# Rows of 1/rms made elementwise from the sums on all partitions, in a hybrid encoder block on one core

## The chip, the core and the metric

The kernel runs on one core of one Trainium2 chip. The metric is the device time of one execution in microseconds (us); the kernel before takes 879.52 us, the median of three runs. The core has a matrix engine (TensorE, in the profile PE, its weight loads PEld), a vector engine (VectorE, DVE), an engine for functions by table (ScalarE, ACT), a general one (GpSimd, POOL) and one that issues DMAs (SyncE, SP). Each works through its own instructions in order and waits on semaphores for the others. On-chip data lie in SBUF; matmul results go to PSUM, which has banks of 128 partitions by 512 fp32 numbers.

## What is computed

One encoder block on x, 512 tokens by 1024 channels, in fp32. The normalisation is what the change touches:

```python
def rms_norm(x, g):
    xf = x.astype(F32)
    y = xf * lax.rsqrt(jnp.mean(xf * xf, axis=-1, keepdims=True) + EPS)   # EPS = 1e-6
    return (y * g.astype(F32)).astype(x.dtype)
```

The block is: h = rms_norm(x); one projection of h gives the inputs of three token mixers and of three merge gates. Mixer A is a bidirectional mLSTM (with a 3-tap convolution and silu on its q and k), B an attention within a neighbourhood, C a cross-attention into rms_norm(mem), with mem of 256 tokens. Each mixer is projected, multiplied by its sigmoid gate, summed, projected again and added to x. Then x plus a convolutional GLU network on rms_norm(x) (2816 hidden channels: a and u are two projections; gelu of the 3-tap convolution of a, times u, projected down), and a last rms_norm.

## The kernel before

**Layout.** Activations are kept with channels on partitions and tokens along the row, so 512 tokens are one row of 512 numbers, a full PSUM bank. The weights come in blocks of 128 by 1024, in the order in which they are used (`BLOCKS`), by DMAs from SP three blocks ahead (`RAW_AHEAD`, L147 and L159). One block ahead, each is split into a high and a low part: ScalarE writes the high part (L195), VectorE subtracts it and gives the low part (L196), each in two halves. A product of fp32 accuracy is then three matmuls, high by high, high by low, low by high (`mm3`, L213 to L215). `proj` (L395) does the 8 channel tiles of one output tile, 24 matmuls of 128x512; its argument `at` runs a function behind a given channel tile.

**The normalisations.** The gain g is multiplied into the activations when these are split. 1/rms depends on the token alone, so it is applied to the projections' results. For results with channels on partitions it has to be a row, the same on all 128 partitions (`rb`, 128x512); for those with tokens on partitions it is a column (`rc`, 128x4, one number for each token). It is made three times: for x, for mem (256 tokens) and for the second norm. The last norm has other code and is not touched.

1. The squares of the channel tiles are summed on 128 partitions: `acc` for x (L381 to L385), `macc` for mem (L485 to L492), `acc2` for the second norm (L1141 to L1145).
2. `two_parts` (L299) splits that sum, and `rstd_cols` (L305) multiplies both parts by a matrix of ones (L310). The result in PSUM holds each token's sum of squares on all 128 partitions.
3. `rstd_cols` then takes, 128 tokens at a time, the diagonal out of it: product with the identity, summed along the row, divided by 1024, epsilon added (L314). POOL raises that to the power -0.5 (L317), which is the column.
4. `row_parts` (L320) splits the column into a high part (ScalarE, L324) and a low part (VectorE, L325) and writes both back as diagonal matrices (L330, 128x128 each).
5. `rstd_row` (L334) multiplies the two by the matrix of ones (L339), which spreads each token's number over all partitions, and ScalarE copies the result out of PSUM (L341): the row.

For x the sums are issued inside the projection `mlk` 0 (L443), the row's matmuls inside `mlk` 1 (L444). The row is first read by `conv` (L456), which multiplies the four accumulated tiles `ps_q` of the mLSTM's q and the first two of its k by it, and goes on with L458 to L460 and the silu (L465, L466). The pool `mmp` has four PSUM banks, all held by `ps_q` up to there; `mlk` 2, the next projection, takes the first that comes free. The pool `atp` has four more (sums, rows, the first two k tiles, and the token tiles of the first `tm` block, L500 to L510). The column of x is multiplied by a constant (L448) and scales what is computed with tokens on partitions (L514 to L526).

For mem the sums are issued after the tile `("o", 1)` (L1035), the diagonals after `("o", 2)` (L1037), the row's matmuls within `("o", 3)` (L1021 to L1025). Row and column are read from the `memk` and `memv` tiles on (L1045, L1057). Around it the steps of the mLSTM run (`step`): decay factors by Exp (L710, L714), products with them (L715, L717), matmuls on these (L725, L727).

For the second norm the sums are issued behind the last channel tile of `ua` 0 (L1305), the row's matmuls within `uu` 1 (L1309). The row is read by `conv` (L456) and once more on POOL (L1319).

**The order.** A scheduler of the language lays out each engine's instructions; `tc.issue_after` holds an instruction behind a named one. The order of the lines is therefore not that of an engine, and a change in one helper can move others' instructions.

Of the kernel before, what the change touches and what calls it, by code (L numbers as in the profile page):

```python
# [11 lines left out]
F32 = mybir.dt.float32  # L12
# [5 lines left out]
P = 128  # L18
S = 512
# [91 lines left out]
def hybrid_block(ctx, tc, xg, xT, memT, wflat, vecs, gbias, nabias, outa, outb, outc):  # L111
# [14 lines left out]
    def nm(s):  # L126
        uid[0] += 1
        return f"{s}_{uid[0]}"
# [4 lines left out]
    def scr(n=512):  # L133
        return sp.tile([P, S], F32, tag="scr", name=nm("s"))[:, :n]

    def tiny(n):
        return tp.tile([P, 32], F32, tag="tiny", name=nm("y"), bufs=12)[:, :n]
# [4 lines left out]
    def atps():  # L142
        return atp.tile([P, 512], F32, tag="at", name=nm("at"))
# [158 lines left out]
        V.tensor_tensor(l, acc, h.bitcast(F32), op=ALU.subtract)  # L302
        return h, l

    def rstd_cols(parts, ntok, tag, n=D):  # L305

        nt = ntok // P
        ps = atps()
        for i in range(2):
            st["mm"] = PE.matmul(ps[:, :ntok], onesr, parts[i], start=i == 0, stop=i == 1).ins  # L310

        v, junk = tiny(nt), scr(P)
        for t in range(nt):
            V.tensor_tensor_reduce(junk, ps[:, t * P:(t + 1) * P], ident, 1.0 / n, EPS, ALU.mult, ALU.add,  # L314
                                   accum_out=v[:, t:t + 1])
        col = cp.tile([P, nt], F32, name=f"rc_{tag}")
        st["pool"] = G.tensor_tensor(col, v, nhalf[:, :nt], op=ALU.pow).ins  # L317
        return col

    def row_parts(col, ntok):  # L320

        nt = ntok // P
        ch, cl = tp.tile([P, 32], F32R, tag="tiny", name=nm("y"), bufs=12)[:, :nt], tiny(nt)
        A.activation(ch, col, AF.Copy)  # L324
        V.tensor_tensor(cl, col, ch.bitcast(F32), op=ALU.subtract)  # L325
        dgs = []
        for c in (ch.bitcast(F32), cl):
            dg = sp.tile([P, S], F32R, tag="scr", name=nm("s"))[:, :ntok]
            for t in range(nt):
                V.tensor_scalar(dg[:, t * P:(t + 1) * P], ident, c[:, t:t + 1], None, op0=ALU.mult)  # L330
            dgs.append(dg)
        return dgs

    def rstd_row(col, ntok, tag, parts=None):  # L334

        dgs = parts or row_parts(col, ntok)
        pb = atps()
        for n, dg in enumerate(dgs):
            PE.matmul(pb[:, :ntok], onesr, dg, start=n == 0, stop=n == 1)  # L339
        rb = cp.tile([P, ntok], F32, name=f"rb_{tag}", tag=f"rb{ntok}", bufs=1)  # L340
        A.activation(rb, pb[:, :ntok], AF.Copy)  # L341
        return rb


# [34 lines left out]
    def x_square(k):  # L379
        if k == 0:  # L380
            A.activation(acc, xk[k], AF.Square)  # L381
        else:
            sq = scr()
            A.activation(sq, xk[k], AF.Square)
            V.tensor_tensor(acc, acc, sq, op=ALU.add)  # L385

    norm = []
    late = []
# [6 lines left out]
    def proj(key, XHs, XLs, n=S, at={}, ps=None):  # L395

        ws = weights(key)
        k0 = 0 if ps is None else 1
        if ps is None:
            ps = mmps()  # L400
        for k in range(k0, KT):
            mm3(ps[:, :n], ws[k][0], ws[k][1], XHs[k], XLs[k], k == 0, k == KT - 1)
            if k == 1:
                flush()
            if k in at:
                at[k]()
        return ps
# [32 lines left out]
                mm3(ps_k[f], kh[:, fs], kl[:, fs], XH[0], XL[0], True, False)  # L440

    xsum = two_parts(acc, S)
    proj(("mlk", 0), XH, XL, ps=ps_k[0], at={1: lambda: norm.append(rstd_cols(xsum, S, "x"))})  # L443
    proj(("mlk", 1), XH, XL, ps=ps_k[1], at={4: lambda: norm.append(rstd_row(norm[0], S, "x"))})  # L444
    rc, rb = norm
    SY.dma_start(gbf, gbias.partition_broadcast(P))
    rcc = cp.tile([P, NT], F32, name="rcc")
    V.tensor_scalar(rcc, rc, C_ML, None, op0=ALU.mult)  # L448
# [31 lines left out]
    def mem_part(kp):  # L480

        t = scr()
        SY.dma_start(t.rearrange("p (k m) -> p k m", k=2), memT[:, 2 * kp:2 * kp + 2, :])
        sq = scr()
        A.activation(sq, t, AF.Square)  # L485
        for i in range(2):
            k = 2 * kp + i
            split_act(MH[k], ML[k], t[:, i * M:(i + 1) * M], vcol("mem_g", k))
            if k == 0:
                V.tensor_tensor(macc, sq[:, :M], sq[:, M:2 * M], op=ALU.add)  # L490
            elif k > 1:
                V.tensor_tensor(macc, macc, sq[:, i * M:(i + 1) * M], op=ALU.add)  # L492

# [517 lines left out]
    gens.append(ml_all())  # L1011

    xq = unit()
    mrbs = []
    for f in range(4):
        ps = proj(("xaq", f), XH, XL)
        V.tensor_tensor(xq[:, f * S:(f + 1) * S], ps, rb, op=ALU.mult)
        mem_part(f)
        step(RB)
    for f in range(4):  # L1020
        def mem_row():  # L1021
            with tc.issue_after(st["mm"]):
                mrbs.append(rstd_row(mrc, M, "m", mparts))

        ps = proj(("o", f), XH, XL, at={1: mem_row} if f == 3 else {})  # L1025
        t = scr()
        V.tensor_tensor(t, ps, rb, op=ALU.mult)
        A.activation(t, t, AF.Tanh, scale=0.5)
        if f == 0:
            so.append(unit())  # L1030
            msum = two_parts(macc, M)
        if f == 1:

            with tc.issue_after(st["mm"]):
                mrc = rstd_cols(msum, M, "m")  # L1035
        if f == 2:
            mparts = row_parts(mrc, M)  # L1037
        V.tensor_scalar(so[0][:, f * S:(f + 1) * S], t, 1.0, None, op0=ALU.add)
        step(RB)
    mrb = mrbs[0]  # L1040
    mkv = unit()
    mk, mv = mkv[:, 0:1024], mkv[:, 1024:2048]
    for f in range(4):
# [90 lines left out]
    for f in range(KT):  # L1134
        xr = scr()
        SY.dma_start(xr, xT[f])
        ps = proj(("out", f), GH, GL)
        V.tensor_tensor(x2[f], ps, xr, op=ALU.add)
        split_act(HH[f], HL[f], x2[f], vcol("ffn_g", f))
        if f == 0:  # L1140
            A.activation(acc2, x2[f], AF.Square)  # L1141
        else:
            sq = scr()
            A.activation(sq, x2[f], AF.Square)
            V.tensor_tensor(acc2, acc2, sq, op=ALU.add)  # L1145


    acc3 = cp.tile([P, S], F32, name="acc_3", tag="acc", bufs=1)
# [140 lines left out]
    for hh in range(2):  # L1289
        gu = [unit(F32R) for _ in range(6)]  # L1290
        UH = [gu[k // 4][:, (k % 4) * S:(k % 4 + 1) * S] for k in range(HF)]
        UL = [gu[3 + k // 4][:, (k % 4) * S:(k % 4 + 1) * S] for k in range(HF)]
        for j in range(HF):
            f = HF * hh + j
            if f == 0:
                wa, wu = weights(("ua", f)), weights(("uu", f))
                pa, pu = mmps(), mmps()
                for k in range(KT):
                    if k < KT - 1:
                        mm3(pa, wa[k][0], wa[k][1], HH[k], HL[k], k == 0, False)  # L1300
                for k in range(KT - 1):
                    mm3(pu, wu[k][0], wu[k][1], HH[k], HL[k], k == 0, False)
                k = KT - 1
                mm3(pa, wa[k][0], wa[k][1], HH[k], HL[k], False, True)
                rc2 = rstd_cols(two_parts(acc2, S), S, "2")  # L1305
                mm3(pu, wu[k][0], wu[k][1], HH[k], HL[k], False, True)
                pa1 = proj(("ua", 1), HH, HL)
                norm2 = []
                pu1 = proj(("uu", 1), HH, HL, at={0: lambda: norm2.append(rstd_row(rc2, S, "2"))})  # L1309
                rb2 = norm2[0]  # L1310
            else:
                pa = pa1 if f == 1 else proj(("ua", f), HH, HL)
            c = conv(pa, rb2, "ffw", "ffb", f, FT)
            sq = scr()
            A.activation(sq, c, AF.Square)
            V.scalar_tensor_tensor(sq, sq, GC, c, op0=ALU.add, op1=ALU.mult)  # L1316
            A.activation(sq, sq, AF.Tanh, scale=GK)  # L1317
            V.scalar_tensor_tensor(c, sq, 1.0, c, op0=ALU.add, op1=ALU.mult)  # L1318
            G.tensor_tensor(c, c, rb2, op=ALU.mult)  # L1319
            if f > 0:  # L1320
                pu = pu1 if f == 1 else proj(("uu", f), HH, HL)
            V.tensor_tensor(c, pu, c, op=ALU.mult)  # L1322
            split_act(UH[j], UL[j], c, 0.5)
        for f in range(KT if hh == 0 else LF - 1):
            ws = weights(("dn", hh, f, 0)) + weights(("dn", hh, f, 1))
            ps = mmps()
            for k in range(HF):
                mm3(ps, ws[k][0], ws[k][1], UH[k], UL[k], k == 0, k == HF - 1)
            V.tensor_tensor(x2[f], ps, x2[f], op=ALU.add)
            if hh == 1:  # L1330
                if f == 0:
                    A.activation(acc3, x2[f], AF.Square)
                else:
                    sq = scr()
                    A.activation(sq, x2[f], AF.Square)
                    G.tensor_tensor(acc3, acc3, sq, op=ALU.add)
                A.activation(x2[f], x2[f], AF.Copy, scale=vcol("fin_g", f))
        if hh == 1:
            last_tiles(UH, UL)
# [114 lines left out]
```

## Time and profile before

| | us |
|---|---|
| median of three runs | 879.52 (879.36 to 879.62) |
| span of the profiled execution | 878.1 |
| TensorE busy | 872.7 |
| VectorE busy | 582.2 |
| ScalarE busy | 451.4 |
| POOL busy | 127.1 |

The span is from the first to the last instruction of the one execution that was profiled; the runs' times hold what lies around it too, some 1.4 us. Times in a timeline count from the start of the span. A line of a timeline is: start, duration, engine, line of the kernel, operation, output <- inputs by the program's names, shapes, count; in brackets how long the engine had been idle, and what ended that. Matmuls overlap: two of 512 columns that follow each other start 0.23 apart though each lasts 0.39.

### The profile page before, as it was taken

To read this page: it belongs to the slowest core of one execution; us is meant where nothing else is said; L and a number is where in the kernel's file an instruction comes from. 1 tells how busy PE (TensorE), PEld (TensorE's weight loads), DVE (VectorE), ACT (ScalarE), POOL (GpSimd) and SP (SyncE) were. 2 spreads that over 40 slices of the span, in tenths; PEclk is the share of its full clock that TensorE was granted. 3 is DMA by queue.
4 is the path that set the end of the run, shared out by engine and by line. 5 is a ranking of instruction groups with operands and counts; after the bars stand their busy time and mean duration, and the time that the engine had idled before them with its cause. 6 is when DMAs were issued, how large, how long until landed. Compare 5 with 4: busy or idle time off the path is not lost.

```text
span 878.1 us, 12238 instructions
## 1 busy us (share of the span) xinstructions
PE 872.7 (99%) x4334; PEld 740.4 (84%) x4334; DVE 582.2 (66%) x1211; ACT 451.4 (51%) x953; POOL 127.1 (14%) x203
## 2 busy tenths in 40 slices
PE   9999999999999999999999999999999999999997
PEld 7898889888888888888888888888888888888897
DVE  7694686775667758898676558776633466666433
ACT  7363555754456658888544435444422344444532
POOL 0101100001072460700000002111100011111011
PEclk9999999999999999999999999999999999999999
DMA  8224643522242354533223432222233322222412
GB/s 280 99 73 140 207 135 97 192 85 90 74 137 87 107 146 131 156 110 130 97 97 109 144 107 94 99 97 96 72 103 101 109 97 97 98 97 87 141 34 96
DMA packets 39421, 99.81 MB, mean 114 GB/s; under 512 B 5688, under 2 KB 13880, under 8 KB 39360
## 3 DMA queue, kind: packets, MB, share of 16 engines
q1 hardware_dynamic: 31568, 92.32, 31.1%
q0 software_dynamic: 7360, 6.32, 3.1%
q8 instruction: 34, 0.56, 0.3%
q10 hardware_dynamic: 432, 0.39, 0.1%
q14 instruction: 27, 0.22, 0.1%
HBM read 94.80 MB, written 4.21 MB: 113 GB/s over the span
## 4 chain that ended last, share of the span: by engine, by line
PE 99%; issue 0%; ACT 0%; DVE 0%; POOLq 0%; POOL 0%; DVEq 0%
PE mm L213 29%; PE mm L215 29%; PE mm L214 29%; PE at L214 2%; PE at L213 2%; PE at L215 2%; PE at L872 1%; PE at L725 1%; PE at L853 1%; PE at L727 1%; PE at L690 1%; PE at L834 0%; PE at L835 0%; PE at L706 0%; PE at L960 0%
## 5 line engine op out<-in xcount | busy, mean ns | idle before, releaser
L213 PE MATMUL mm<-u,wh 128*128 128x512 f32 (+1 forms) x1072 | 415.6, 388 | 0.0
L215 PE MATMUL mm<-u,wl 128*128 128x512 f32 (+1 forms) x1072 | 412.2, 385 | 0.0
L214 PE MATMUL mm<-u,wh 128*128 128x512 f32 (+1 forms) x1072 | 411.8, 384 | 0.0
L195 ACT ACTIVATE wh<-wr 128x512 fp32r<-128x512 f32 (+2 forms) x298 | 184.1, 622 | 234.4 <-PE mm L214 188.1
L196 DVE TENSOR_TENSOR wl<-wr,wh 128x512 fp32r<-128x512 f32 (+3 forms) x300 | 203.1, 678 | 92.4 <-ACT wh L195 85.8
L215 PEld LDWEIGHTS mm<-u,wl 128*128 128x128 f32 x1072 | 201.5, 188 | 40.1
L214 PEld LDWEIGHTS mm<-u,wh 128*128 128x128 f32 x1072 | 201.8, 188 | 38.8
L213 PEld LDWEIGHTS mm<-u,wh 128*128 128x128 f32 x1072 | 201.8, 188 | 38.2
L1319 POOL TENSOR_TENSOR s<-s,rb 128x512 f32<-128x512 f32 x22 | 38.3, 1739 | 250.0 <-DVE s L1318 238.1
L538 POOL DMA_DIRECT2D u<-nav_d x128 | 62.2, 512 | 66.5 <-PE at L872 22.5
L219 ACT ACTIVATE u<-s 128x512 fp32r<-128x512 f32 x26 | 16.4, 630 | 57.5 <-DVE s L1322 56.1
L1322 DVE TENSOR_TENSOR s<-mm,s 128x512 f32<-128x512 f32 x22 | 15.2, 691 | 25.1 <-POOL s L1319 25.1
L458 ACT ACTIVATE s<-pad,vec 128x512 f32<-128x512 f32 x30 | 24.4, 813 | 9.5 <-DVE pad L456 9.5
L459 DVE SCALAR_TENSOR_TENSOR s<-pad,vec,s 128x512 f32<-128x512 f32 x30 | 23.6, 786 | 6.1 <-ACT s L458 6.0
L220 DVE SCALAR_TENSOR_TENSOR u<-s,u 128x512 fp32r<-128x512 f32 x26 | 18.0, 691 | 14.1 <-ACT u L219 14.0
L1318 DVE SCALAR_TENSOR_TENSOR s<-s,s 128x512 f32<-128x512 f32 x22 | 15.2, 692 | 13.4 <-ACT s L1317 13.3
L317 POOL TENSOR_TENSOR rc<-y,nhalf 128x4 f32<-128x4 f32 x1 | 1.0, 1032 | 152.9 <-DVE y L314 152.9
L460 DVE SCALAR_TENSOR_TENSOR s<-pad,vec,s 128x512 f32<-128x512 f32 x30 | 22.5, 750 | 0.7
L1317 ACT ACTIVATE s<-s 128x512 f32<-128x512 f32 x22 | 13.9, 632 | 15.1 <-DVE s L1316 15.1
L456 DVE TENSOR_TENSOR pad<-mm,rb 128x512 f32<-128x512 f32 x22 | 15.1, 691 | 7.3 <-PE mm L215 6.5
L213 PE MATMUL mm<-wh,u 128*128 128x512 f32 x48 | 18.9, 394 | 0.0
L214 PE MATMUL mm<-wl,u 128*128 128x512 f32 x48 | 18.8, 392 | 0.0
(315 smaller groups left out, 1028.4 us busy)
## 6 DMA issues: line engine op xcount, KB each, us to landing
wr<-wflat SPq DMA_DIRECT2D x141, 512.0 KB, 3.3
nab<-nabias SPq DMA_DIRECT2D x16, 256.0 KB, 2.7
u<-nav_d POOLq DMA_DIRECT2D x128, 32.0 KB, 2.6
s<-xT SPq DMA_DIRECT2D x15, 256.0 KB, 3.9
wr<-wflat SPq DMA_DIRECT2D x14, 192.0 KB, 2.3
nav_d<-nv POOLq DMA_DIRECT2D x8, 256.0 KB, 2.4
R<-rd SPq DMA_DIRECT2D x8, 256.0 KB, 3.9
wr<-wflat SPq DMA_DIRECT2D x2, 544.0 KB, 3.3
```

The lines of the kernel that those rows point to most:

```text
L195: A.activation(h[:, u:v], src, AF.Copy)
L196: V.tensor_tensor(l[:, u:v], src, h[:, u:v].bitcast(F32), op=ALU.subtract)
L213: PE.matmul(ps, lh, rh, start=start, stop=False)
L214: PE.matmul(ps, lh, rl, start=False, stop=False)
L215: st["mm"] = PE.matmul(ps, ll, rh, start=False, stop=stop).ins
L219: A.activation(h, src, AF.Copy, scale=scale)
L220: V.scalar_tensor_tensor(l, src, scale, h.bitcast(F32), op0=ALU.mult, op1=ALU.subtract)
L458: A.activation(t1, pad[:, 0:512], AF.Identity, scale=vcol(w, i), bias=vcol(b, i))
L459: V.scalar_tensor_tensor(t1, pad[:, 1:513], vcol(w, n + i), t1, op0=ALU.mult, op1=ALU.add)
L460: V.scalar_tensor_tensor(t1, pad[:, 2:514], vcol(w, 2 * n + i), t1, op0=ALU.mult, op1=ALU.add)
L538: G.dma_start(vw[r * 32:(r + 1) * 32, i * 256:(i + 1) * 256], nav_v[hf, r, CW[b]:CW[b] + 32, hp * 256:(hp + 1) * 256])
L1319: G.tensor_tensor(c, c, rb2, op=ALU.mult)
```

## The change

The row no longer comes from the column. The matmuls with ones (`square_sums`, new) leave each token's sum on all partitions; `rstd_wide` (new) reads them there and works on all 128x512 numbers: ScalarE takes the logarithm of the mean, then the exponential of -0.5 times that, and VectorE makes one Newton step, y (1.5 - 0.5 s y y / n), from the sums s and the estimate y, in three instructions. `row_parts` and `rstd_row` go, with their splits, diagonals, matmuls and the copy. `rstd_cols` stays for x and mem, from the same sums; the second norm's column, which only its row needed, goes with its power on POOL. Epsilon is no longer added to the diagonal: it enters the partial sums, once per partition, as EPS * 1024 / 128, for which the accumulations become instructions with a scalar.

```diff
-    def rstd_cols(parts, ntok, tag, n=D):
-
-        nt = ntok // P
+    def square_sums(parts, ntok):
+
         ps = atps()
         for i in range(2):
             st["mm"] = PE.matmul(ps[:, :ntok], onesr, parts[i], start=i == 0, stop=i == 1).ins
-
+        return ps
+
+    def rstd_cols(ps, ntok, tag, n=D):
+
+        nt = ntok // P
         v, junk = tiny(nt), scr(P)
         for t in range(nt):
-            V.tensor_tensor_reduce(junk, ps[:, t * P:(t + 1) * P], ident, 1.0 / n, EPS, ALU.mult, ALU.add,
+            V.tensor_tensor_reduce(junk, ps[:, t * P:(t + 1) * P], ident, 1.0 / n, 0.0, ALU.mult, ALU.add,
                                    accum_out=v[:, t:t + 1])
...
-    def row_parts(col, ntok):
...
-    def rstd_row(col, ntok, tag, parts=None):
...
+    def rstd_wide(ps, ntok, tag, n=D):
+
+        v, y = scr(ntok), scr(ntok)
         rb = cp.tile([P, ntok], F32, name=f"rb_{tag}", tag=f"rb{ntok}", bufs=1)
-        A.activation(rb, pb[:, :ntok], AF.Copy)
+        A.activation(v, ps[:, :ntok], AF.Ln, scale=1.0 / n)
+        A.activation(y, v, AF.Exp, scale=-0.5)
+        V.scalar_tensor_tensor(v, ps[:, :ntok], -0.5 / n, y, op0=ALU.mult, op1=ALU.mult)
+        V.tensor_tensor(v, v, y, op=ALU.mult)
+        V.scalar_tensor_tensor(rb, v, 1.5, y, op0=ALU.add, op1=ALU.mult)
         return rb
...
-            V.tensor_tensor(acc, acc, sq, op=ALU.add)
+            V.scalar_tensor_tensor(acc, acc, EPS * D / P if k == 1 else 0.0, sq, op0=ALU.add, op1=ALU.add)
...
-    proj(("mlk", 0), XH, XL, ps=ps_k[0], at={1: lambda: norm.append(rstd_cols(xsum, S, "x"))})
-    proj(("mlk", 1), XH, XL, ps=ps_k[1], at={4: lambda: norm.append(rstd_row(norm[0], S, "x"))})
-    rc, rb = norm
+    def x_norm():
+        ps = square_sums(xsum, S)
+        norm.extend([rstd_wide(ps, S, "x"), rstd_cols(ps, S, "x")])
+
+    proj(("mlk", 0), XH, XL, ps=ps_k[0], at={1: x_norm})
+    proj(("mlk", 1), XH, XL, ps=ps_k[1])
+    rb, rc = norm
...
-        def mem_row():
-            with tc.issue_after(st["mm"]):
-                mrbs.append(rstd_row(mrc, M, "m", mparts))
-
-        ps = proj(("o", f), XH, XL, at={1: mem_row} if f == 3 else {})
+        ps = proj(("o", f), XH, XL)
...
             with tc.issue_after(st["mm"]):
-                mrc = rstd_cols(msum, M, "m")
-        if f == 2:
-            mparts = row_parts(mrc, M)
+                mps = square_sums(msum, M)
+            mrb, mrc = rstd_wide(mps, M, "m"), rstd_cols(mps, M, "m")
...
-                rc2 = rstd_cols(two_parts(acc2, S), S, "2")
+                rb2 = rstd_wide(square_sums(two_parts(acc2, S), S), S, "2")
...
-                pu1 = proj(("uu", 1), HH, HL, at={0: lambda: norm2.append(rstd_row(rc2, S, "2"))})
-                rb2 = norm2[0]
+                pu1 = proj(("uu", 1), HH, HL)
```

`macc` and `acc2` get epsilon in the same way as `acc`.

More of the change, by code (lines that the diff above doesn't have):

```diff
@@ L318, in rstd_cols @@
         return col
-    def row_parts(col, ntok):
[L322 to L332, printed above, removed]
-    def rstd_row(col, ntok, tag, parts=None):
[L336 to L339, printed above, removed]
-        rb = cp.tile([P, ntok], F32, name=f"rb_{tag}", tag=f"rb{ntok}", bufs=1)
-        A.activation(rb, pb[:, :ntok], AF.Copy)
+    def rstd_wide(ps, ntok, tag, n=D):
+        v, y = scr(ntok), scr(ntok)
+        rb = cp.tile([P, ntok], F32, name=f"rb_{tag}", tag=f"rb{ntok}", bufs=1)
+        A.activation(v, ps[:, :ntok], AF.Ln, scale=1.0 / n)
[3 more added lines that the diff above has]
+        V.scalar_tensor_tensor(rb, v, 1.5, y, op0=ALU.add, op1=ALU.mult)
         return rb
@@ L489, in mem_part @@
             if k == 0:
-                V.tensor_tensor(macc, sq[:, :M], sq[:, M:2 * M], op=ALU.add)
+                V.scalar_tensor_tensor(macc, sq[:, :M], EPS * D / P, sq[:, M:2 * M], op0=ALU.add, op1=ALU.add)
             elif k > 1:
@@ L1013, in hybrid_block @@
     xq = unit()
-    mrbs = []
     for f in range(4):
@@ L1034, in hybrid_block @@
             with tc.issue_after(st["mm"]):
-                mrc = rstd_cols(msum, M, "m")
-        if f == 2:
-            mparts = row_parts(mrc, M)
+                mps = square_sums(msum, M)
+            mrb, mrc = rstd_wide(mps, M, "m"), rstd_cols(mps, M, "m")
         V.tensor_scalar(so[0][:, f * S:(f + 1) * S], t, 1.0, None, op0=ALU.add)
         step(RB)
-    mrb = mrbs[0]
     mkv = unit()
@@ L1144, in hybrid_block @@
             A.activation(sq, x2[f], AF.Square)
-            V.tensor_tensor(acc2, acc2, sq, op=ALU.add)
+            V.scalar_tensor_tensor(acc2, acc2, EPS * D / P if f == 1 else 0.0, sq, op0=ALU.add, op1=ALU.add)
     acc3 = cp.tile([P, S], F32, name="acc_3", tag="acc", bufs=1)
@@ L1304, in hybrid_block @@
                 mm3(pa, wa[k][0], wa[k][1], HH[k], HL[k], False, True)
-                rc2 = rstd_cols(two_parts(acc2, S), S, "2")
+                rb2 = rstd_wide(square_sums(two_parts(acc2, S), S), S, "2")
                 mm3(pu, wu[k][0], wu[k][1], HH[k], HL[k], False, True)
                 pa1 = proj(("ua", 1), HH, HL)
-                norm2 = []
-                pu1 = proj(("uu", 1), HH, HL, at={0: lambda: norm2.append(rstd_row(rc2, S, "2"))})
-                rb2 = norm2[0]
+                pu1 = proj(("uu", 1), HH, HL)
             else:
```

## The prediction

> **What bounds the kernel now.** I read the page first: engine shares, then the 40 slices, then the chain that ended last. The columns of the first line are busy time, share of the span and instructions.
>
> ```profile
> span 878.1 us, 12238 instructions
> ...
> PE 872.7 (99%) x4334; PEld 740.4 (84%) x4334; DVE 582.2 (66%) x1211; ACT 451.4 (51%) x953; POOL 127.1 (14%) x203
> ...
> PEclk9999999999999999999999999999999999999999
> ...
> PE 99%; issue 0%; ACT 0%; DVE 0%; POOLq 0%; POOL 0%; DVEq 0%
> ```
>
> TensorE is busy for 99% of the span, in every slice at full clock, and the chain that ended last is 99% TensorE. No other engine sets the time as long as it delivers before a matmul needs its result. Two things only can move the time: matmuls that go, each at its pace in the stream, and a matmul that is made to wait. So I look at what goes, and then at each of the three places (x, mem, second norm) for the first matmul that could wait.
>
> **What goes from TensorE.** Each of the three `rstd_row` calls issues two matmuls (L339). The timeline of TensorE at the three places, columns start, duration, what:
>
> ```profile
> 29.13 0.62 PE L310 MATMUL at<-s,onesr 128*128 128x512 f32 x2
> ...
> 36.38 0.62 PE L339 MATMUL at<-s,onesr 128*128 128x512 f32 x2
> 36.84 0.39 PE L213 MATMUL at<-u,wh 128*128 128x512 f32 x1
> ...
> 38.88 0.39 PE L213 MATMUL mm<-u,wh 128*128 128x512 f32 x1
> ```
>
> ```profile
> 139.00 0.40 PE L339 MATMUL at<-s,onesr 128*128 128x256 f32 x2
> 139.23 0.40 PE L213 MATMUL mm<-u,wh 128*128 128x512 f32 x1
> ```
>
> ```profile
> 526.62 0.62 PE L339 MATMUL at<-s,onesr 128*128 128x512 f32 x2
> 527.07 0.39 PE L213 MATMUL mm<-u,wh 128*128 128x512 f32 x1
> ```
>
> The matmuls overlap, so the price of a pair is the distance to the next start: 36.84 - 36.38 = 0.46, 139.23 - 139.00 = 0.23, 527.07 - 526.62 = 0.45. Together **1.14 us** leave the bounding engine. The two matmuls of the sums (L310) stay, and the built order of TensorE is otherwise the same: nothing else is moved on it, and the DMA issues on SP and POOL stay, but for one weight load on SP that moves by one place. SP issues each weight block three blocks ahead, so that costs nothing; were it late by its neighbour's issue, it would still be ahead by more than a block of 24 matmuls.
>
> **What is added, and where it queues.** A row is now made by ScalarE and VectorE from the sums: Ln, Exp, and three VectorE instructions. In the built order the table of ScalarE is switched before each Ln and back before the next Exp or Tanh, so six switches are added. The only one in the trace of before stands at the start:
>
> ```profile
> 1.66 1.28 ACT L267 ACT_TABLE_LOAD   x1 [1.66 <-PEq L1441]
> 2.96 0.20 ACT L267 ACTIVATE first<-const-float32-1.0 128x2 f32<-128x2 f32 x1
> ```
>
> It took 1.28 us, and the next instruction began 0.02 later. This trace shows none behind a working ScalarE, so its price there is open. From below 1.28 stands. From above I take two such loads, 2.56, as if the engine emptied for as long as it loads; nothing in the rows reaches that far. I take 1.28, the row itself, because nothing stands between that load and its neighbours but 0.02 to 0.03 us.
>
> The Trainium skill ("ScalarE: Activation LUTs", section "What ACT_TABLE_LOAD costs") gives 1283 ns for the load, which the row confirms, and about 1380 ns more for a drain, 2.66 us for every switch; no such drain stands beside the one load here, and by that price the sum below would be about +1.9 us or more instead of a gain. The same page ("Table sets: the hidden batching unit") says that one set holds both exp and ln, so that Ln and then Exp need one load; by that the x chain below would end 1.28 earlier and the whole 1.14 would be kept. The built order has two loads per row all the same.
>
> **The x row, the place that decides.** ScalarE and VectorE around it, before:
>
> ```profile
> 28.42 0.63 ACT L195 ACTIVATE wh<-wr 128x512 fp32r<-128x512 f32 x1 [2.09 <-PE mm L214]
> 30.96 0.63 ACT L195 ACTIVATE wh<-wr 128x512 fp32r<-128x512 f32 x1 [1.91 <-PE at L214]
> ...
> 33.63 0.63 ACT L195 ACTIVATE wh<-wr 128x512 fp32r<-128x512 f32 x1 [1.08 <-PE at L214]
> ...
> 37.03 0.60 ACT L341 ACTIVATE rb_x<-at 128x512 f32<-128x512 f32 x1 [0.73 <-PE at L339]
> ```
>
> ```profile
> 29.90 0.29 DVE L314 CUSTOM_DVE_ANT_0 s<-at,ident 128x128 f32<-128x128 f32 x1
> 30.12 0.08 DVE L314 DVE_READ_ACCUMULATOR2_ANT y<- 128x1 f32 x1
> 30.23 0.29 DVE L314 CUSTOM_DVE_ANT_0 s<-at,ident 128x128 f32<-128x128 f32 x1
> ...
> 33.14 1.83 DVE L330 TENSOR_SCALAR s<-ident,y 128x128 fp32r<-128x128 f32 x8
> 34.89 0.68 DVE L196 TENSOR_TENSOR wl<-wr,wh 128x512 fp32r<-128x512 f32 x1
> 36.34 0.69 DVE L196 TENSOR_TENSOR wl<-wr,wh 128x512 fp32r<-128x512 f32 x1 [0.77 <-ACT wh L195]
> 37.66 1.29 DVE L456 TENSOR_TENSOR pad<-mm,rb_x 128x512 f32<-128x512 f32 x2 [0.63 <-ACT rb_x L341]
> ```
>
> The first thing that reads the row is L456, which empties the first bank of `ps_q`. The four banks of `mmp` are all held by `ps_q`, so the first matmul of `mlk` 2 (38.88) waits for that bank: before, it came free at 37.66 + 0.69 = 38.35, with 0.53 to spare. Now the new chain:
>
> - The sums end at 29.13 + 0.62 = 29.75. ScalarE is idle there (its last split ended at 29.05). Load 29.78 to 31.06. Ln 31.08 to 31.68, priced as the row's eviction L341, 0.60 for the same shape out of PSUM.
> - In the built order a weight split (L195, 0.63) stands between; it begins some 0.1 before Ln ends, and ends at 32.22. Load to 33.50. Exp, 0.62 as the L195 rows (same shape, no per-partition operand), 33.52 to 34.14. The next split slips from 33.63 to 34.05; TensorE reads it in the second half of `mlk` 2, after 41, so that is hidden.
> - VectorE: in the built order the three row instructions, the four pieces of the column sums (L314) and one low split (L196) stand before L456. Two L456 take 1.29 for 0.69 each, so an instruction of 128x512 occupies 0.61 before the next begins; a piece with its read occupies 30.23 - 29.90 = 0.33. From 34.17: 4 x 0.61 + 4 x 0.33 = 3.76, so L456 begins at 37.93 and the bank is free at 38.62.
>
> TensorE would be there at 38.88 - 0.46 = 38.42, and with 0.04 for the signal (L341 began 0.03 after its matmuls, 37.03 against 36.38 + 0.62) it waits until 38.66: **0.24 us of a new wait**. With 2.56 a switch the bank is free 2.56 later and the wait is 2.80. With an unhindered chain it is nothing.
>
> Behind it VectorE is later than before. From the page's groups, the power on POOL that the column vector needs, and a VectorE instruction with a per-partition scalar (busy, mean ns):
>
> ```profile
> L459 DVE SCALAR_TENSOR_TENSOR s<-pad,vec,s 128x512 f32<-128x512 f32 x30 | 23.6, 786 | 6.1 <-ACT s L458 6.0
> ...
> L317 POOL TENSOR_TENSOR rc<-y,nhalf 128x4 f32<-128x4 f32 x1 | 1.0, 1032 | 152.9 <-DVE y L314 152.9
> ```
>
> The delay: L456 by 0.27, a wait for POOL's power (L317, 1.03 us, which now starts after 37.9 and holds the instruction between the two L456) by about 0.45, and a low split that now stands behind instead of ahead by 0.61, in sum 1.3. Who waits: the fourth token tile of the first `tm` block, which takes the bank that the second key tile leaves.
>
> ```profile
> 51.99 0.69 DVE L456 TENSOR_TENSOR pad<-at,rb_x 128x512 f32<-128x512 f32 x1
> ```
>
> ```profile
> 54.24 0.29 PE L213 MATMUL at<-wh,u 128*128 128x272 f32 x1
> ```
>
> Before, 54.24 - 52.68 = 1.56 to spare; now about 54.02 against 53.98. I count 0, and up to 0.3 in the range. The banks of the sums are held until 37.9 instead of 31.2, but one bank fewer is taken, and the scratch tiles are two more and two fewer.
>
> **The mem row.** Its two loads, Ln (0.38) and Exp come behind the splits at 131.47 (below: 130.33 + 1.14). Nothing needs the row before the `memk` tiles at 146.
>
> ```profile
> 130.33 1.14 ACT L195 ACTIVATE wh<-wr 128x512 fp32r<-128x512 f32 x2
> 133.07 0.63 ACT L1028 ACTIVATE s<-s 128x512 f32<-128x512 f32 x1 [1.59 <-DVE s L1027]
> ...
> 139.43 0.38 ACT L341 ACTIVATE rb_m<-at 128x256 f32<-128x256 f32 x1
> ```
>
> ```profile
> 138.67 0.41 DVE L715 TENSOR_TENSOR E<-E,at 128x256 f32<-128x256 f32 x1
> ```
>
> ```profile
> 143.56 0.39 PE L725 MATMUL at<-u,E 128*128 128x129 f32 x2
> ...
> 145.93 0.36 PE L213 MATMUL mm<-u,wh 128*128 128x256 f32 x1
> ```
>
> Load to 132.75, Ln to 133.15, load to 134.45, then the Tanh of 133.07: 1.4 late, and with it Exp (to 135.5). The row's three instructions, two pieces, a low split and L1027 (0.69, between them) end near 138.4, and L715 follows at about its old 138.7. TensorE reads that product at 143.56. No wait; the cover is 4.5 us.
>
> **The second norm's row.** Sums at 519.37, as L310 in the rows below; ScalarE: split to 519.97, load to 521.25, Ln to 521.85, split to 522.4, load to 523.7, Exp to 524.3. VectorE: two row instructions and a split, then the last one that waits for its neighbour: 0.61 + 0.61 + 0.69 + 0.69 = 2.60, so L456 begins near 526.95.
>
> ```profile
> 519.34 0.63 ACT L195 ACTIVATE wh<-wr 128x512 fp32r<-128x512 f32 x1 [2.03 <-PE mm L214]
> ...
> 527.27 0.60 ACT L341 ACTIVATE rb<-at 128x512 f32<-128x512 f32 x1 [0.73 <-PE at L339]
> ```
>
> ```profile
> 527.90 1.29 DVE L456 TENSOR_TENSOR pad<-mm,rb 128x512 f32<-128x512 f32 x2 [0.63 <-ACT rb L341]
> ```
>
> ```profile
> 531.83 0.39 PE L213 MATMUL mm<-u,wh 128*128 128x512 f32 x1
> ```
>
> That is 0.95 earlier than 527.90, while TensorE is earlier by 0.45 here: the row gains. Its bank is wanted by the tile that began at 531.83, 3 us later, so no wait even at 2.56 a switch. The epsilon as a scalar operand of the accumulations costs VectorE 0.1 us each at most (0.69 against the 0.79 of L459, which has one by partition); they end microseconds before the sums' matmuls, and TensorE sits between with other work.
>
> **Sum.** -0.46 - 0.23 - 0.45 + 0.24 = **-0.90 us**, span 877.2. The span stands 1.4 below the median of the runs (879.52); the start and end are not touched, so I subtract from the median: **878.6 us**, 0.1% faster.
>
> **The rivals.**
> - *All is kept*: the bank is free in time, if ScalarE or VectorE gains 0.24 on my chain. -1.14, 878.4. For it: each term is rounded up by some hundredths. Against: the chain has ten links.
> - *A switch costs more behind a working engine*, but less than double: wait 0.5 to 2.2, so 878.9 to 880.6. For it: no row has that case. Against: the 0.02 beside the one load.
> - *The switches take over* (the other side): a switch of 2.5 or more. Bank free near 41.2, wait 2.8, net +1.66, and the mem row, now 2.6 later, runs into the products that TensorE reads from 143.56 on, for up to 1 us: 881.2 to 882.2, I say 881.7. It turns the sign at a wait of 1.14, 0.45 more per switch than the row shows, and passes 0.2% at a wait of 2.9. The skill's price named above lies here.
> - *The rows do not come earlier at all*: the columns still go through POOL in x and mem, and the row of x is later, 38.0 against 37.6. This is in my sum already; where nothing waits for a row its lateness costs nothing.
>
> **Chances.** About 0.2%, 1.76 us, is what a measurement of this kernel can tell from no change: below 877.76 is faster, above 881.28 slower. My forecast 0.48, all kept 0.17, a dearer switch 0.16: together within 0.2%, 0.81. The switches take over 0.15: slower. Something faster that no row shows 0.04. The range goes from all kept with the spread of the runs (879.36 to 879.62), 878.2, to the double switch without the mem row, 881.2; it leaves out the rest, under 2 in 10.
>
> **What would show it.** Right: no L339 matmuls; six table loads of about 1.3 with the neighbours close; L456 near 37.9; a gap of 0.1 to 0.5 in the matmuls near 38.4 and none near 54, 145 or 531. Wrong: an idle stretch of ScalarE beside a load; a gap over 1 us at 38.4; any gap in the matmuls after the mem row; TensorE waiting for a DMA or a bank that I have not named.

## The result, and the profile after

| | before | after |
|---|---|---|
| median, measured together on one chip | 879.26 (879.04 to 879.86) | 878.16 (877.75 to 878.78) |
| span of the profiled execution | 878.1 | 876.3 |

The ratio is 0.9987, its 95% interval 0.9981 to 0.9993: 1.10 us faster (0.6 to 1.7). That is within the 0.2% that the prediction took for what a measurement can tell; the interval still lies wholly below 1. The kernel before, measured 21 times beside the changed one, has a median 0.26 below that of the three runs that the prediction started from (879.52).

The page of the changed kernel, the lines that answer to those of before:

```profile
span 876.3 us, 12208 instructions
...
PE 870.6 (99%) x4328; PEld 738.3 (84%) x4328; DVE 581.7 (66%) x1189; ACT 459.1 (52%) x959; POOL 126.2 (14%) x202
...
PEclk9999999999999999999999999999999999999999
...
PE 98%; issue 0%; DMA 0%; ACT 0%; SPq 0%; DVE 0%; POOLq 0%; POOL 0%; DVEq 0%
```

TensorE has six matmuls fewer, 4328 for 4334, and bounds the kernel as before. ScalarE does 7.7 us more, about as much as six table loads of 1.28 (7.68), and nothing waits for that: the chain that ended last is still TensorE's.

TensorE's timeline at four places: the sums of x, the first matmul of `mlk` 2 with the one ahead of it, and the two matmuls that followed the removed pairs of mem and of the second norm.

```profile
28.57 0.62 PE L309 MATMUL at<-s,onesr 128*128 128x512 f32 x2
...
37.68 0.39 PE L215 MATMUL at<-u,wl 128*128 128x512 f32 x1
37.90 0.40 PE L213 MATMUL mm<-u,wh 128*128 128x512 f32 x1
...
138.03 0.39 PE L213 MATMUL mm<-u,wh 128*128 128x512 f32 x1
...
525.19 0.39 PE L213 MATMUL mm<-u,wh 128*128 128x512 f32 x1
```

The matmul at 37.90 begins 0.22 after the one ahead of it, the ordinary pace: **the wait of 0.24 us that the prediction put there did not come.** In the trace of before the same four matmuls began at 29.13, 38.88, 139.23 and 527.07. After is earlier by 0.56, 0.98, 1.20 and 1.88. The first 0.56 arose in the start-up, ahead of the sums' matmuls. It is no gain that can be put down to the change: in the experiments below, which share the changed kernel's code up to there, the first table load of the x row begins anywhere from 28.97 to 29.96. At the x row follow 0.42, at the mem row 0.22; of the 0.68 up to the third, 0.45 is the pair, and the rest, 0.23, comes in steps too small to name over 380 us. So the spans' difference of 1.8 is no measure of the change; the medians' 1.10 is, and the three pairs add up to 1.14.

ScalarE of the changed kernel at the x row, then at the mem row:

```profile
29.27 1.28 ACT L327 ACT_TABLE_LOAD   x1 [0.79 <-PE at L309]
30.56 0.60 ACT L327 ACTIVATE s<-at 128x512 f32<-128x512 f32 x1
31.06 0.62 ACT L195 ACTIVATE wh<-wr 128x512 fp32r<-128x512 f32 x1
31.70 1.28 ACT L328 ACT_TABLE_LOAD   x1
32.99 0.63 ACT L328 ACTIVATE s<-s 128x512 f32<-128x512 f32 x1
...
130.80 1.28 ACT L327 ACT_TABLE_LOAD   x1
132.10 0.38 ACT L327 ACTIVATE s<-at 128x256 f32<-128x256 f32 x1
132.50 1.28 ACT L1017 ACT_TABLE_LOAD   x1
133.79 0.63 ACT L1017 ACTIVATE s<-s 128x512 f32<-128x512 f32 x1
```

A load behind a working ScalarE takes 1.28 too, and its neighbours stand 0.01 to 0.02 away: 31.06 + 0.62 = 31.68, load at 31.70, Exp at 32.99. VectorE from the end of Exp to the first product with the row (L450, which was L456), then that product for the second key tile, L709 (was L715) in the mem row, and the first product of the second norm:

```profile
33.66 0.69 DVE L329 SCALAR_TENSOR_TENSOR s<-at,s 128x512 f32<-128x512 f32 x1 [1.25 <-ACT s L328]
34.27 0.28 DVE L317 CUSTOM_DVE_ANT_0 s<-at,ident 128x128 f32<-128x128 f32 x1
34.47 0.08 DVE L317 DVE_READ_ACCUMULATOR2_ANT y<- 128x1 f32 x1
34.47 0.69 DVE L330 TENSOR_TENSOR s<-s,s 128x512 f32<-128x512 f32 x1
...
36.91 0.69 DVE L450 TENSOR_TENSOR pad<-mm,rb_x 128x512 f32<-128x512 f32 x1
...
52.18 0.69 DVE L450 TENSOR_TENSOR pad<-at,rb_x 128x512 f32<-128x512 f32 x1
...
137.43 0.41 DVE L709 TENSOR_TENSOR E<-E,at 128x256 f32<-128x256 f32 x1
...
525.55 1.29 DVE L450 TENSOR_TENSOR pad<-mm,rb 128x512 f32<-128x512 f32 x2
```

A piece of the column sums (one `rstd_cols` step of 128 tokens: the diagonal's product and sum, then the read of the accumulator) occupies 34.47 - 34.27 = **0.20** between two instructions of the row, not 0.33: its read of the accumulator and the next instruction start together. The bank is free at 36.91 + 0.69 = 37.60.

### The profile page after: what moved, and what is told of

The parts are those of the page before. It is cut to its first block, busy times and chain, and to the rows that moved or that the text cites. A ratio compares the mean times of both kernels' runs of the same rounds, so it can differ in the third digit from the quotient of the medians.

```text
span 876.3 us, 12208 instructions
## 1 busy us (share of the span) xinstructions
PE 870.6 (99%) x4328; PEld 738.3 (84%) x4328; DVE 581.7 (66%) x1189; ACT 459.1 (52%) x959; POOL 126.2 (14%) x202
## 4 chain that ended last, share of the span: by engine, by line
PE 98%; issue 0%; DMA 0%; ACT 0%; SPq 0%; DVE 0%; POOLq 0%; POOL 0%; DVEq 0%
PE mm L213 29%; PE mm L215 29%; PE mm L214 29%; PE at L214 2%; PE at L213 2%; PE at L215 2%; PE at L866 1%; PE at L719 1%; PE at L847 1%; PE at L721 1%; PE at L684 1%; DMA wr<-wflat 0%; PE at L828 0%; PE at L829 0%; PE at L700 0%
## 5 line engine op out<-in xcount | busy, mean ns | idle before, releaser
L450 DVE TENSOR_TENSOR pad<-mm,rb 128x512 f32<-128x512 f32 x22 | 15.1, 690 | 6.2 <-PE mm L215 6.1
L213 PE MATMUL mm<-wh,u 128*128 128x512 f32 x48 | 18.9, 394 | 0.0
L215 PE MATMUL mm<-wh,u 128*128 128x512 f32 x48 | 18.7, 390 | 0.0
```

The costliest lines, as they stand in the source:

```text
L213: PE.matmul(ps, lh, rh, start=start, stop=False)
L215: st["mm"] = PE.matmul(ps, ll, rh, start=False, stop=stop).ins
```

## The experiments

The theory: the change takes six matmuls (1.14 us) from the bounding engine, and all else is covered; the x row is the only place with little cover. The rivals: the gain is not the matmuls'; a table switch costs more than 1.28; the three rows have equal cover; or the x row has none. All kernels are the changed one with one edit. Times of before beside them: 879.40 (879.45 beside those run once).

**The six matmuls put back.** `spare_pair` issues two matmuls of ones with an activation into a bank of `atp` that nobody reads, where the rows' pairs stood; the rows stay elementwise. `pairs3` issues each pair three times.

```diff
+    def spare_pair(src, ntok):
+        for _ in range(1):          # pairs3: range(3)
+            pb = atps()
+            for i in range(2):
+                PE.matmul(pb[:, :ntok], onesr, src, start=i == 0, stop=i == 1)
-    proj(("mlk", 1), XH, XL, ps=ps_k[1])
+    proj(("mlk", 1), XH, XL, ps=ps_k[1], at={4: lambda: spare_pair(XH[0], S)})
```

(The same at `("o", 3)` with 256 columns and at `uu` 1.)

> The changed kernel, with the six matmuls put back where the row's pairs stood, on data that lie ready and into banks that nobody reads. Theory (the gain is the six matmuls' places in TensorE's stream, 0.46 + 0.23 + 0.45): it goes back to the kernel before, ratio to it 1.000 within 0.0005, and the next matmul starts 0.45, 0.23 and 0.45 us behind each pair. Rival (the gain comes from what VectorE, ScalarE or POOL no longer do, or from the start): it stays near 0.9987.

> The same with each pair put back three times, eighteen matmuls. Theory: 3 x 1.14 = 3.42 us above the changed kernel, 2.28 above the kernel before, ratio to it 1.0026. Rival (TensorE has slack there, or the gain is elsewhere): below 1.0010.

Measured: `pairs1` 879.32, ratio to before 0.9999 (0.9990 to 1.0008). The time is that of before again, 1.16 above the changed kernel, and no execution of `pairs1` (879.01 to 880.01) is as short as the longest of the changed kernel (878.78): the gain is the matmuls' time. `pairs3` 882.48, ratio 1.0035 (1.0022 to 1.0048): 3.08 above before, where two more pairs at each place than before has ask for 2 x 1.14 = 2.28. The timelines of `pairs3` at the x row, TensorE and VectorE, show the rest:

```profile
36.57 0.63 PE L316 MATMUL at<-u,onesr 128*128 128x512 f32 x2
37.74 1.21 PE L316 MATMUL at<-u,onesr 128*128 128x512 f32 x4 [0.55 <-DVE y L323]
```

```profile
37.40 0.28 DVE L323 CUSTOM_DVE_ANT_0 s<-at,ident 128x128 f32<-128x128 f32 x1
37.61 0.08 DVE L323 DVE_READ_ACCUMULATOR2_ANT y<- 128x1 f32 x1
```

The second pair starts 37.74 - 36.57 = 1.17 after the first instead of 0.46: it waits 0.71 until the last piece has read the sums, whose bank it takes. 2.28 + 0.71 = 2.99. So this kernel ran into a bank shortage of its own, and it confirms the price of a pair only with that wait taken off; the interval of its ratio, 1.9 to 4.2 us, could not tell 2.28 from 2.99. The sums' bank is now held until the last piece has read it, and only the missing pair makes room for that.

**Two more switches in the x row, or in the other two.** Between Ln and Exp stand an Exp, an Ln and a copy of two columns, which Exp overwrites.

```diff
         A.activation(v, ps[:, :ntok], AF.Ln, scale=1.0 / n)
+        if tag in ("x",):           # delay_m2: ("m", "2")
+            t = tiny(4)
+            A.activation(t[:, 0:2], v[:, 0:2], AF.Exp, scale=-0.5)
+            A.activation(t[:, 2:4], t[:, 0:2], AF.Ln)
+            A.activation(y[:, 0:2], t[:, 2:4], AF.Copy)
```

> The changed kernel with two more table switches (and three instructions of 128x2) between Ln and Exp of the x row alone: its chain is some 2.56 + 0.5 = 3.1 us longer. Theory (in the changed kernel the bank of ps_q is free 0.3 us before mlk 2 wants it, and beyond that cover every delay is a wait of TensorE): a gap of about 2.8 us in the matmuls ahead of mlk 2, 881.0 us, ratio to the kernel before 1.0019. It also shows the price of a switch behind a working ScalarE four times: 1.28 to 1.3 each, by the drain rival 2.7. Rival (VectorE makes the lateness up, as the row has no reader that TensorE waits for): no gap, 0.9987.

> The same two more switches in the mem row and in the second norm's row, none more in the x row. Theory (cover of about 4.5 and 3.9 us there): no gap in the matmuls beyond 0.15 us, ratio 0.9987 as the changed kernel. Rival (from the forecast's last case: a mem row later by 2.6 us runs into the products that TensorE reads): a gap of up to 1 us between 138 and 146 us, ratio up to 1.0000.

`delay_x`: 881.51, ratio 1.0030 (1.0021 to 1.0040). ScalarE, then TensorE and the first product with the row:

```profile
29.12 1.28 ACT L327 ACT_TABLE_LOAD   x1 [0.79 <-PE at L309]
...
31.55 1.28 ACT L330 ACT_TABLE_LOAD   x1
...
33.07 1.28 ACT L331 ACT_TABLE_LOAD   x1
34.37 0.20 ACT L331 ACTIVATE y<-y 128x2 f32<-128x2 f32 x1
...
34.82 1.28 ACT L333 ACT_TABLE_LOAD   x1
```

```profile
37.53 0.39 PE L215 MATMUL at<-u,wl 128*128 128x512 f32 x1
40.86 0.47 PE L213 MATMUL mm<-u,wh 128*128 128x512 f32 x1 [2.94 <-DVE pad L455]
```

```profile
40.03 0.69 DVE L455 TENSOR_TENSOR pad<-mm,rb_x 128x512 f32<-128x512 f32 x1
```

Four loads in a row take 1.28 each; 33.07 + 1.28 = 34.35, and the next instruction begins at 34.37: no price beyond the load. The added work shifts the last load by 34.82 - 31.55 = 3.27, and TensorE's next matmul comes 40.86 - 37.53 - 0.23 = 3.10 late. Of 3.27 only 0.17 was covered. The gap expected was 2.8: the three small instructions took 3.27 - 2.56 = 0.71, not 0.5, and the cover is 0.17, not 0.3.

`delay_m2`: 878.08, ratio to before 0.9983 (0.9975 to 0.9992), the time of the changed kernel. Four more loads of 1.28 are in its timeline of ScalarE, for example

```profile
134.77 1.28 ACT L331 ACT_TABLE_LOAD   x1
...
522.47 1.28 ACT L331 ACT_TABLE_LOAD   x1
```

and no matmul waits behind them. The mem row and the second norm's have room for two more loads, 2.56 us, and the instructions between them; the x row has room for 0.17. The same two switches cost 3 us or nothing, by the place.

**How much cover the x row has.** One more pass of ScalarE between Ln and Exp, 128 or 512 columns wide:

```diff
+        if tag == "x":
+            A.activation(y[:, :512], v[:, :512], AF.Copy)   # hold_128: 128 columns
```

> The changed kernel with one more ScalarE pass of 128x128 between Ln and Exp of the x row (it writes scratch that Exp overwrites). By the rows of the changed kernel (Ln of 128x256 0.38, of 128x512 0.60) such a pass occupies some 0.25 us, an estimate. Theory (the piece of the column sums was priced too high; the first bank comes free 0.30 us ahead of the matmul that wants it, less 0.04 for the signal): the extra 0.25 uses the cover up and no gap over 0.05 us stands ahead of the first matmul of `mlk` 2. Rival (the forecast's chain, by which the bank is late already and the place has no cover): a gap of 0.25 or more there.

> The same with a pass of 128x512, 0.60 to 0.63 us by the rows of that shape. Theory (cover 0.26 to 0.30): a gap of 0.30 to 0.37 us ahead of the first matmul of `mlk` 2, and none elsewhere. Rival one (no cover, the forecast's chain): 0.6 or more, up to 0.84. Rival two (cover much larger than the 0.30 between the end of the pad and the matmul, because something else sets the start of that matmul): no gap.

Each was run once (878.37 and 878.58); the reading is the trace's. `hold_128`: the first load, the pad, the last matmul of `mlk` 1 and the first of `mlk` 2:

```profile
29.42 1.28 ACT L327 ACT_TABLE_LOAD   x1 [0.79 <-PE at L309]
```

```profile
37.26 0.69 DVE L452 TENSOR_TENSOR pad<-mm,rb_x 128x512 f32<-128x512 f32 x1
```

```profile
37.83 0.39 PE L215 MATMUL at<-u,wl 128*128 128x512 f32 x1
38.10 0.47 PE L213 MATMUL mm<-u,wh 128*128 128x512 f32 x1
38.40 0.40 PE L214 MATMUL mm<-u,wh 128*128 128x512 f32 x1
```

The same of `hold_512`:

```profile
29.30 1.28 ACT L327 ACT_TABLE_LOAD   x1 [0.79 <-PE at L309]
```

```profile
37.47 0.69 DVE L452 TENSOR_TENSOR pad<-mm,rb_x 128x512 f32<-128x512 f32 x1
```

```profile
37.71 0.39 PE L215 MATMUL at<-u,wl 128*128 128x512 f32 x1
38.30 0.47 PE L213 MATMUL mm<-u,wh 128*128 128x512 f32 x1 [0.20 <-DVE pad L452]
```

From the first load to the end of the pad it is 8.33 us in the changed kernel (29.27 to 37.60), 8.53 in `hold_128`, 8.86 in `hold_512`. The gaps ahead of `mlk` 2, beyond the pace of 0.23, are 0.04 and 0.36. So 0.20 later costs 0.04, and 0.53 later costs 0.36: cover 0.16 and 0.17, as in `delay_x`. The expectation of 0.26 to 0.30 was too high, because the signal is dearer than the 0.04 it took: in `hold_512` the bank is free at 38.16 and the matmul starts at 38.30, 0.14 later (0.15 in `hold_128`). Of the 0.30 between 37.60 and 37.90 in the changed kernel, 0.14 is that signal. The rival without cover would have had the whole 0.20 as a gap in `hold_128`, and falls. That both gaps lie in the forecast (no more than 0.05, and 0.30 to 0.37) is luck in part: the passes delayed the chain less than was taken (0.20 for 0.25, 0.53 for 0.60), and the cover was smaller too.

**Two pieces fewer ahead of the row's reader.** `delay_x` with the columns called after `mlk` 1; in the built order two pieces then stand behind the first product.

```diff
-        norm.extend([rstd_wide(ps, S, "x"), rstd_cols(ps, S, "x")])
+        norm.extend([rstd_wide(ps, S, "x"), ps])
-    rb, rc = norm
+    rb, xps = norm
+    rc = rstd_cols(xps, S, "x")
```

> The kernel with two more table switches in the x row, which had a gap of 3.10 us, now with the column sums called after the second `mlk` projection: in the built order two of the four pieces then stand behind the first product with the row instead of ahead of it; all else of VectorE's chain to it is the same. If a piece between the row's instructions costs 0.20 (the rows of the changed kernel), the gap is 3.10 - 0.40 = 2.70; if it costs the 0.33 of the forecast, 3.10 - 0.66 = 2.44; if the pieces hide behind the row's own latency and are free, 3.10.

> The same kernel as delay_x_late, timed. Its profiled execution had 882.28 although its gap (2.69) was shorter than that of delay_x (3.10, 881.12 in its profiled execution): in it the granted clock was 0.50 to 0.60 from 41 to 44 us, behind the gap. Theory one (the clock drops in some executions only, by where the gap falls in time, and then costs some 1.7 us: half speed for 3.4 us): the executions fall in two groups, near 880.8 (878.16 + 2.69) and near 882.5, and the median lies in one of them. Theory two (this kernel's longer stretch behind the gap is of its own order of instructions): all executions near 882.3, and the clock low in this profile too.

```profile
37.38 0.39 PE L215 MATMUL at<-u,wl 128*128 128x512 f32 x1
40.30 0.47 PE L213 MATMUL mm<-u,wh 128*128 128x512 f32 x1 [2.52 <-DVE pad L456]
...
42.24 0.63 PE L213 MATMUL mm<-u,wh 128*128 128x512 f32 x1
42.66 0.63 PE L214 MATMUL mm<-u,wh 128*128 128x512 f32 x1
```

The gap of `delay_x_late` in this timeline is 40.30 - 37.38 - 0.23 = 2.69, 0.41 less than that of `delay_x`: 0.20 for each piece, as in the rows. The 0.33 of the forecast (2.44) and free pieces (3.10) fall.

The time was another matter: 882.28 in the profiled execution, and 881.66 (880.75 to 882.76, ratio 1.0026, 1.0017 to 1.0035) when timed, though the gap is shorter than that of `delay_x`. The view of stretches of 1 us of `delay_x_late`, columns after the stretch: length, each engine's busy share and count, granted clock, DMA share and GB/s.

```profile
41.00:42.00 1.00, 1.00 (x4) 0.74 (x4) 0.85 (x3) 0.58 (x2) 0.75 (x1) 0.60 0.44 169
42.00:43.00 1.00, 1.00 (x4) 0.81 (x3) 0.23 (x2) 0.00 (x0) 1.00 (x2) 0.50 0.00 0
43.00:44.00 1.00, 1.00 (x4) 0.72 (x3) 1.00 (x3) 0.00 (x0) 1.00 (x3) 0.50 0.00 0
44.00:45.00 1.00, 1.00 (x5) 0.82 (x4) 1.00 (x3) 0.77 (x2) 0.34 (x4) 0.70 0.00 0
```

Behind the gap the granted clock falls to 0.50, and the matmuls follow each other at 0.42 instead of 0.23; by these shares some 1.7 us are lost (0.4 + 0.5 + 0.5 + 0.3). The second profile of this kernel shows it too; the one profile of `delay_x` (gap 3.10, 881.12) does not: its clock is 1.00 throughout.

The mean granted clock of each execution, which is on record with its time, tells more. Of the eleven timed executions of `delay_x_late`, the seven from 880.75 to 881.73 have 1.000, and the four from 882.06 to 882.76 have 0.997 or 0.998. Of the nine of `delay_x`, the six from 881.10 to 881.63 have 1.000, and the other three, 882.89, 883.06 and 884.74, have 0.998, 0.998 and 0.995. So both kernels lose clock in some executions, and these are the longer ones: that is theory one, and theory two falls. Theory one had its groups near 880.8 and 882.5; parted by their clock, they have medians of 881.42 and 882.47. Why the lower one is 0.6 above its forecast stays open: at full clock `delay_x` takes 881.41, so the gap that is 0.41 shorter in the trace does not show in the times.

## Why the prediction was right or wrong

- *Three pairs, 0.46 + 0.23 + 0.45 = 1.14.* Right. Put back, they restore the time (`pairs1`); in the trace the steps are 0.42 at x and 0.22 at mem.
- *A table switch at 1.28.* Right in every load of every run, behind a working ScalarE as well. The price of 2.66 with a drain that the Trainium skill gives ("ScalarE: Activation LUTs", section "What ACT_TABLE_LOAD costs") is not borne out here: the neighbours stand 0.02 away, and two more switches with three small instructions cost 3.27. The two rivals with dearer switches fall with it. They were right that a longer chain makes a wait at the x row: `delay_x` made one.
- *The new wait of 0.24 at `mlk` 2.* **This step failed.** Its chain ran 8.15 from the first load to the product (29.78 to 37.93); the trace has 7.64 (29.27 to 36.91). The link that was mis-sized is the piece of the column sums: 0.33 four times, taken from rows in which pieces follow each other. Between other instructions a piece occupies 0.20 (seen in the rows, and by moving two pieces in `delay_x_late`), which is 0.52 less in all. A second link erred the other way: the signal from the bank, emptied by VectorE, to the matmul is 0.14; the 0.04 was taken from a ScalarE instruction behind matmuls. The rest agrees to some hundredths. So in place of the wait there are 0.16 to spare (37.90 - 37.60 - 0.14), which the three delays measure as 0.16 or 0.17. It was the rival *all is kept* (chance 0.17) that came, by a gain on VectorE. The trace of before already held the price of 0.20, in a row that the prediction did not use: at the mem row a piece stood ahead of another instruction there and occupied 133.15 - 132.94 = 0.21:

```profile
132.94 0.28 DVE L314 CUSTOM_DVE_ANT_0 s<-at,ident 128x128 f32<-128x128 f32 x1
133.15 0.09 DVE L314 DVE_READ_ACCUMULATOR2_ANT y<- 128x1 f32 x1
133.15 0.42 DVE L715 TENSOR_TENSOR E<-E,at 128x256 f32<-128x256 f32 x1
```

- *"The row of x is later, 38.0 against 37.6".* Not so; what is later is the first product with it. The row is complete at 35.28 + 0.69 = 35.97, 1.93 ahead of `mlk` 2; before, it was at 37.03 + 0.60 = 37.63, 1.25 ahead. The product begins 0.99 ahead of `mlk` 2, where it was 1.22, because two pieces and a split now stand between.
- *Epsilon in the accumulations, up to 0.1 each.* It cost nothing that the trace shows: 0.68 each for x, before and after.
- *The second key tile and the fourth token tile.* The product with the row, L450, came 1.17 later against TensorE than before (52.18 against 51.99, with TensorE 0.98 ahead); 1.3 was forecast. No matmul waits there.
- *The mem row.* From the splits' end to the Tanh 3.00 were forecast; 130.79 to 133.79 is 3.00. No wait, even with two more switches.
- *The second norm.* The forecast had 6.98 from the first load to the product; the trace has it from 518.51 to 525.55, 7.04. No wait, even with two more switches.
- *The base.* The sum was made from the three runs' 879.52. Beside the changed kernel, before had 879.26. The forecast of 878.6 is 0.44 above 878.16: 0.24 from the wait and 0.26 from the base, less 0.06. The interval of the medians (0.6 to 1.7 us) could not have told a gain of 0.90 from 1.14; the trace without a gap and the delays do.

## What to carry to other kernels

Where TensorE is busy for 99%, as here, an edit is worth the matmuls that it takes away, less the waits at places where the new chain has no cover. That cover can be measured by adding known delays and reading the gap in the trace, far below what the time can resolve. Take an instruction's price from rows with the same neighbours: a piece with an accumulator read cost 0.33 ahead of its like and 0.20 ahead of other work, and the trace of before had both. Before adding work to a row, find which of its places has room: here two more table switches were free at two of them and cost 3.1 us at the third.

## What was not expected of the hardware

- The clock: a TensorE idle for 2.52 us was followed, in both profiles of `delay_x_late`, by some 3 us at half the granted clock; in the profile of `delay_x`, idle for 2.94, it was not, though three of that kernel's nine executions had a lower mean clock. The Trainium skill ("TensorE: Matmul & The Clock Gate", Part 1, section "What's actually happening") puts the drop behind an idle window of about 3.4 us that runs free of the kernel. The drop came here after less idle time than that, in a matmul stream that had resumed 0.8 us before. That some executions lose clock and others do not agrees with a window that runs free, but no run here shows the window.
- A matmul behind a wait starts slowly: in `hold_128` the first of `mlk` 2 lasts 0.47 instead of 0.39, and the next begins 0.30 later instead of 0.23, another 0.07 beyond the gap.
